# Out-projection accumulated onto a ScalarE copy in PSUM, two early products in row tiles, and a reworked end of the FFN

## The chip, the cores and the metric

The kernel runs on one core of one Trainium2 chip. The metric is the device time of one launch in microseconds. The kernel before took 1280.64 us (median of three runs, 1278.71 to 1283.99).

## The reference

One layer of a streaming encoder over 1024 tokens of width 1024, all in float32: sandwich RMSNorm, a token mixer with two head groups (a gated DeltaNet and a latent attention) whose outputs are concatenated, one output projection, and a squared-ReLU MLP with 4096 hidden columns. The part that the change touches is the second half of the layer:

```python
mixed = jnp.concatenate([o_gdn, o_mla], axis=-1) @ w_out[l]
x = x + rms_norm(mixed, mix_post_norm[l])
h = rms_norm(x, ffn_pre_norm[l])
f = jnp.square(jax.nn.relu(h @ w_up[l])) @ w_down[l]
x = x + rms_norm(f, ffn_post_norm[l])
```

## The kernel before, in words

Every float32 matrix product is done as three fp32r products (`mm3`, lines 207 to 209): each operand is split into a high part (a cast on ScalarE) and a low part (the difference, on VectorE). The tokens are eight blocks of 128, `t` = 0 to 7. TensorE's lines in the trace are mostly those of `mm3`, so the stages are told apart by tile names: `ps_out` is the out-projection, `ps_h2T` the transposes of its normalised rows, `ps_up` and `ps_dn` the two halves of the FFN.

**Out-projection.** The DeltaNet's share of it is computed during the attention and kept in SBUF as `part[t]`. What is left for a block is the attention's share: for each half of 512 columns four pairs, that is 12 matmuls, into a PSUM bank (`out_pairs`). `out_add` then adds the bank to `part[t]` on VectorE (line 1172) and squares the sum on ScalarE into the bank, with the row sums as a by-product (line 1173). Blocks 0 and 1 (`early`) are done at the end of the attention; blocks 2 to 7 take their banks from a pool of four (`psC`, tag `out`). `out_proj(t)` goes on with the norm: the sum of squares, the reciprocal root by a Sqrt on ScalarE and a Newton step in small VectorE operations (lines 155 to 172), the scaling by `rpost` (line 1245), the residual's add (1246), its store to `d_x1`, a second sum of squares on ScalarE (1249), and the scaling by `rffn` (1251). The residual `xt` shares a ring of six tiles (tag `g`) with other tiles.

**First half of the FFN.** It runs on a 2x2 scheme with seven products of half-size blocks in place of eight (the sums and differences T1 to T4 of the rows and S1 to S4 of the weights). `ffn_in(t)` transposes a block's rows on TensorE into one of two banks, and casts and splits them (`put`, lines 1268, 1273 and 1274). The products with the rows' first blocks, B11 and B21, need only token blocks 0 to 3; for every even `p` they are taken ahead as `filler(p)`, between the transposes of blocks 4 to 7, and their results are stored to DRAM. Each filler loads a block of `w_up` into a raw tile (`raw_of`: a ring of three, every fourth from the ring `g`), which stays in use until the filler's second result is stored. All these loads are chained in program order on SyncE's queue (`load_chained`, line 183). Row tiles, a ring of 16 (`mtile`, tag `m`), hold `part`, the attention's rows and later T2 and T4; they come free as blocks 4 to 7 are transposed. `up_pair(p)` then does the remaining products.

**Second half of the FFN.** The 56 steps (seven products, in the order 1, 7, 6, 5, 4, 3, 2, over eight blocks of hidden columns each) accumulate in four banks, one per pair of token blocks; `evict` adds a product to the rows `R` when its eight steps are done. In products 5, 4, 3 and 2 a half of the rows becomes final: it is squared on ScalarE (line 1570) and multiplied by the gain on GpSimd (`gains`, 1573). `final(t)` loads the residual `x1t` from DRAM into one of two tiles (1577), computes the root, and for each half scales and adds on VectorE (1583) and stores. In the last product the last `LASTU` steps are done block by block, so that the first blocks can be evicted while the others still accumulate.

The order of the instructions on each engine isn't that of the program text: a scheduler lists them by readiness on a simulated timeline and by program order among the ready ones, and the tiles' slots and semaphores follow from it. An engine then executes its list in that fixed order.

Of the kernel before, what the change touches and what calls it, by code (L numbers as in the profile page):

```python
# [8 lines left out]
F32 = mybir.dt.float32  # L9
F32R = mybir.dt.float32r  # L10
I32 = mybir.dt.int32
AF = mybir.ActivationFunctionType
ALU = mybir.AluOpType
# [4 lines left out]
P = 128  # L18
T = 1024
D = 1024  # L20
KT = D // P
NT = T // P
HALF = 512
# [4 lines left out]
NPAIR = MH // 2  # L28
# [76 lines left out]
def build(tc, a, out):  # L105
    nc = tc.nc
    mm = nc.tensor.matmul
# [7 lines left out]
    cp = pool(const_stack, "const")  # L115
# [14 lines left out]
    def psum(name, tag="ps"):  # L130
        return pp[0].tile([P, HALF], F32, name=name, tag=tag, bufs=pp[1][tag])
# [8 lines left out]
    ones = cp.tile([P, P], F32, name="ones")  # L140
    nc.vector.memset(ones, 1.0)
    cols = cp.tile([P, NCOL], F32, name="cols")
    cp.tile([P, 48], F32, name="edge_c")
    cur = [cp]

    def col(base, k):
# [2 lines left out]
    def small(shape, name, bufs=2):  # L149
        return cur[0].tile([P] + list(shape), F32, name=name, tag=name, bufs=bufs)  # L150
# [31 lines left out]
    def load_chained(dst, src):  # L182
        ld = nc.sync.dma_start(dst, src).ins
        if last_load:
            after(ld, last_load[0], "loads in the order of use")
        last_load[:] = [ld]
# [19 lines left out]
    def mm3(ps, lhs, rhs, start, stop, **kw):  # L206
        mm(ps, lhs[0], rhs[0], start=start, stop=False, **kw)  # L207
        mm(ps, lhs[0], rhs[1], start=False, stop=False, **kw)  # L208
        mm(ps, lhs[1], rhs[0], start=False, stop=stop, **kw)  # L209

    def cut(pair, *idx):
        return tuple(t[idx] for t in pair)
# [20 lines left out]
    d_x1 = scratch("d_x1", NT, P, D)  # L233
# [7 lines left out]
    R = ExitStack()  # L241
# [759 lines left out]
    first = pool(const_stack, "first")  # L1001
# [4 lines left out]
    mixT, gmix, part, mp = [None] * NPAIR, {}, [], []  # L1006
# [10 lines left out]
    def mtile(name, dt=F32R):  # L1017
        return mp[0].tile([P, T], dt, name=name, tag="m", bufs=16)
# [105 lines left out]
    def out_cols(w, i):  # L1124
        return cut(w[i // 2], slice(None), slice((i % 2) * HALF, (i % 2 + 1) * HALF))
# [36 lines left out]
                nc.scalar.copy(part[t][:, n * HALF : (n + 1) * HALF], ps)  # L1162
                yield

    def out_pairs(ps, t, n, pairs):

        for p in pairs:
            mm3(ps, cut(mixT[p], slice(None), slice(t * P, (t + 1) * P)), out_cols(w[n], p), p == 0, p == NPAIR - 1)

    def out_add(ps, t, n, ss):  # L1170
        h = part[t][:, n * HALF : (n + 1) * HALF]
        nc.vector.tensor_tensor(h, h, ps, op=ALU.add)
        nc.scalar.activation(ps, h, AF.Square, accum_out=ss[:, n : n + 1])

    early, ss1 = {}, {}
# [9 lines left out]
    for i in range(len(units) + LAG + 1):  # L1185
# [4 lines left out]
        if i < len(units):  # L1190
            h, q = units[i]
# [7 lines left out]
        if i >= LAG + 1:  # L1199
            h, q = units[i - LAG - 1]  # L1200
            if q % 2:
                attend(h, q // 2)
        if i == 58:
            w = [[stream(a["w_out"][n, 2 + k], spare=mix_pair if n and k else None) for k in range(2)] for n in range(2)]
# [7 lines left out]
    L.close()  # L1212
    psum_pool("psC", out=4, tr=2, ps=2)


    L = ExitStack()
    bp = pool(L, "blocks")
# [6 lines left out]
    gb = gtile("gpost")  # L1224
# [7 lines left out]
    def out_proj(t):  # L1232
        h = part[t]
        xt = gtile("xt")
        nc.sync.dma_start(xt, a["x"][t * P : (t + 1) * P, :])
        if t not in early:
            ss1[t] = small([2], "ss1")
            for n in range(2):
                ps = psum("ps_out", "out")
                out_pairs(ps, t, n, range(NPAIR))  # L1240
                out_add(ps, t, n, ss1[t])
        ss = ss1[t]
        nc.vector.tensor_scalar(ss[:, 0:1], ss[:, 0:1], ss[:, 1:2], None, op0=ALU.add)
        r = rstd_of(ss[:, 0:1], D, "rpost")
        nc.vector.scalar_tensor_tensor(h, h, r, gb, op0=ALU.mult, op1=ALU.mult)
        nc.vector.tensor_add(xt, xt, h)
        nc.scalar.dma_start(d_x1[t], xt)
        ss2 = small([1], "ss2")
        nc.scalar.activation(h, xt, AF.Square, accum_out=ss2)
        r2 = rstd_of(ss2, D, "rffn")  # L1250
        nc.vector.scalar_tensor_tensor(h, xt, r2, gf, op0=ALU.mult, op1=ALU.mult)
# [65 lines left out]
    def raw_of(src):  # L1317
        raws[0] += 1
        r = gtile("raw") if raws[0] % 4 == 3 else raw_tile()
        load_chained(r, src)  # L1320
        return r
# [22 lines left out]
        return p % 2 == 0  # L1344

    def filler(p):
        x = raw_of(a["w_up"][2 * p])
        w = split_of(x)
        yield
        ps = psum("ps_up")  # L1350
        for k in range(4):
            mm3(ps, k_slice(w, 0, k), moving(B11, k), k == 0, k == 3)
            if k == 1:
                yield
        nc.scalar.copy(x[:, first_half], ps)
        nc.scalar.dma_start(d_p1[p // 2], x[:, first_half])
        yield
        for k in range(4):
            mm3(ps, k_slice(w, 1, k), moving(B21, k), False, k == 3, skip_group_check=True)
            if k == 1:  # L1360
                yield
        square_of = x[:, second_half]
        nc.scalar.activation(square_of, ps, AF.Relu)
        nc.scalar.activation(square_of, square_of, AF.Square)
        nc.scalar.dma_start(act_block(p, 0), square_of)
        yield
# [185 lines left out]
    ep = pool(L, "down")  # L1552
# [11 lines left out]
    ssf = {}  # L1564
# [7 lines left out]
    def gains(t, s):  # L1572
        nc.gpsimd.tensor_tensor(R[t][:, s], R[t][:, s], gb2[:, s], op=ALU.mult)  # L1573

    def final(t):
        x1t = ep.tile([P, D], F32, name="x1t", tag="x1t", bufs=2)
        nc.sync.dma_start(x1t, d_x1[t])
        s1 = small([1], "ssr")
        nc.vector.tensor_tensor(s1, ssf[t][:, 0:1], ssf[t][:, 1:2], op=ALU.add)
        r = rstd_of(s1, D, "rfin")  # L1580
        for n, eng in enumerate((nc.sync, nc.scalar)):
            s = slice(n * HALF, (n + 1) * HALF)
            nc.vector.scalar_tensor_tensor(x1t[:, s], R[t][:, s], r, x1t[:, s], op0=ALU.mult, op1=ALU.add)
            eng.dma_start(out[t * P : (t + 1) * P, s], x1t[:, s])

    def add(dst, x, ps):
# [2 lines left out]
    def evict(i, t):  # L1589
        ps, r1, r2 = bank[t], R[t], R[t + 4]  # L1590
        a1, a2, b1, b2 = r1[:, first_half], r1[:, second_half], r2[:, first_half], r2[:, second_half]
        if i == 1:
            nc.scalar.copy(a1, ps)
        elif i == 7:
            add(b1, a1, ps)
        elif i == 6:
            add(a2, a1, ps)
            add(b1, b1, ps)
        elif i == 5:
            add(b2, b1, ps)  # L1600
            add(a2, a2, ps)
            squares(t + 4, HALF, D, 1)
            gains(t + 4, second_half)
        elif i == 4:
            add(b1, b1, ps)
            squares(t + 4, 0, HALF, 0)
            gains(t + 4, first_half)
            final(t + 4)
        elif i == 3:
            add(a2, a2, ps)  # L1610
            squares(t, HALF, D, 1)
            gains(t, second_half)
        else:
            add(a1, a1, ps)
            squares(t, 0, HALF, 0)
            gains(t, first_half)
            final(t)

    LASTU = 2
    for n in range(2):  # L1620
        d_prepare(n)
    for n, (i, u) in enumerate(steps):
# [79 lines left out]
```

## Time and profile before

| | us |
|---|---|
| median of three runs | 1280.64 |
| profiled execution, its own time | 1280.36 |
| its span, first to last instruction | 1278.6 |
| TensorE busy | 1222.9 (96%) |
| VectorE busy | 903.9 (71%) |
| ScalarE busy | 651.9 (51%) |
| GpSimd busy | 163.4 (13%) |
| mean granted TensorE clock | 0.985 of full speed |

Times in the trace are microseconds from the span's start. PE is TensorE, DVE VectorE, ACT ScalarE, POOL GpSimd, SP SyncE; a letter q behind a name is that engine's queue of DMA issues and waits. The granted clock is in parts of 2.4 GHz. A matmul's row is its own latency; successive matmuls overlap, so the pitch from start to start tells the rate.

### The profile page before, as it was taken

Reading aid. Unit: us, or ns where it says so; the run is one execution under the profiler, and the core shown is the slowest. Engines: PE = TensorE matmul, PEld = TensorE weight load, DVE = VectorE, ACT = ScalarE, POOL = GpSimd, SP = SyncE. Lnnn points to the kernel's source line nnn. Section 1 sums busy time; section 2 is a strip of 40 time slices with the busy share of each in tenths; the row PEclk is TensorE's granted clock in tenths of the full one; section 3 lists DMA queues with packets and bytes.
Section 4 is the critical chain, followed back from the end, with each engine's and each line's share of the span. In section 5 each row is a group of like instructions: output and inputs, shape, how many; then the busy total and the mean of one; then the engine's idle time right before and its main releaser. Section 6 shows DMA issues by size and latency. Waiting matters only on the chain.

```text
span 1278.6 us, 17685 instructions
## 1 busy us (share of the span) xinstructions
PE 1222.9 (96%) x6224; PEld 1035.5 (81%) x6224; DVE 903.9 (71%) x1779; ACT 651.9 (51%) x1189; POOL 163.4 (13%) x152
## 2 busy tenths in 40 slices
PE   7999999999889999999898999999999999999995
PEld 6978888899778878887686888888887888888884
DVE  7678889546556785686976777677656786776744
ACT  6567643425645786774555544444445433344431
POOL 1011011220044553430000000000000000011021
PEclk9999999999989999999898999999999999999998
DMA  5114535736342511124444455455449984555902
GB/s 233 47 61 149 186 119 194 214 86 176 97 139 87 161 50 31 42 67 148 157 164 158 148 201 196 162 206 188 174 154 410 365 295 148 193 165 202 343 19 98
DMA packets 111217, 205.71 MB, mean 161 GB/s; under 512 B 33557, under 2 KB 51989, under 8 KB 111130
## 3 DMA queue, kind: packets, MB, share of 16 engines
q1 hardware_dynamic: 94848, 176.09, 41.1%
q10 hardware_dynamic: 16282, 28.50, 6.0%
q8 instruction: 49, 0.80, 0.3%
q14 instruction: 38, 0.31, 0.1%
HBM read 143.07 MB, written 61.49 MB: 160 GB/s over the span
## 4 chain that ended last, share of the span: by engine, by line
PE 60%; DVE 5%; DMA 3%; ACT 2%; issue 1%; POOL 1%; SPq 0%; DVEq 0%; ACTq 0%; POOLq 0%
PE ps_up L207 8%; PE ps_up L209 8%; PE ps_up L208 8%; PE ps_dn L208 8%; PE ps_dn L209 8%; PE ps_dn L207 8%; PE ps_PT L1061 2%; PE ps_out L207 2%; PE ps_out L208 1%; PE ps_out L209 1%; PE ps_o L1080 1%; PE ps_sc L207 1%; PE ps_o L1079 1%; PE ps_sc L208 1%; PE ps_sc L209 1%
## 5 line engine op out<-in xcount | busy, mean ns | idle before, releaser
L1573 POOL TENSOR_TENSOR rows<-rows,gpost 128x512 f32<-128x512 f32 x16 | 23.9, 1512 | 654.8 <-ACT junk L1570 654.8
L209 PE MATMUL ps_proj<-hThi,wlo 128*128 128x512 f32 x192 | 75.1, 395 | 1.2 <-DVE wlo L199 1.2
L207 PE MATMUL ps_proj<-hThi,whi 128*128 128x512 f32 x192 | 76.0, 396 | 0.0
L208 PE MATMUL ps_proj<-hTlo,whi 128*128 128x512 f32 x192 | 76.0, 396 | 0.0
L1065 DVE TENSOR_TENSOR PTlo<-ps_PT,PThi 128x512 fp32r<-128x512 f32 (+2 forms) x96 | 52.0, 550 | 20.0 <-ACT PThi L1064 19.3
L1064 ACT CAST PThi<-ps_PT 128x512 fp32r<-128x512 f32 (+2 forms) x96 | 45.4, 481 | 29.7 <-PE ps_PT L1061 28.1
L1505 DVE TENSOR_TENSOR dlo<-draw,dhi 128x1024 fp32r<-128x1024 f32 x35 | 44.7, 1301 | 22.0 <-ACT dhi L1504 21.9
L208 PE MATMUL ps_dn<-dlo,dhi 128*128 128x512 f32 x144 | 56.0, 389 | 0.0
L209 PE MATMUL ps_dn<-dhi,dlo 128*128 128x512 f32 x144 | 56.0, 389 | 0.0
L207 PE MATMUL ps_dn<-dhi 128*128 128x512 f32 x144 | 55.5, 389 | 0.0
L1325 ACT CAST whi<-raw 128x1024 fp32r<-128x1024 f32 (+1 forms) x29 | 26.3, 906 | 54.7 <-PE ps_up L208 48.9
L1035 ACT ACTIVATE Pt<-ps_sc,nm 128x896 f32<-128x896 f32 (+3 forms) x64 | 48.0, 749 | 11.8 <-DVE nm L1033 7.6
L1504 ACT CAST dhi<-draw 128x1024 fp32r<-128x1024 f32 x35 | 36.1, 1048 | 34.1 <-issue 13.8
L1061 PE MATMUL ps_PT<-ident,Pt 128*128 128x128 f32 x288 | 46.6, 276 | 2.4 <-DVE PTlo L1065 1.2
L1033 DVE TENSOR_REDUCE nm<-ps_sc 128x1 f32<-128x896 f32 (+3 forms) x64 | 47.8, 750 | 1.2
L1040 POOL TENSOR_TENSOR Pt<-Pt,rs 128x128 f32<-128x128 f32 (+4 forms) x40 | 35.4, 885 | 89.1 <-DVE rs L1038 65.1
L199 DVE TENSOR_TENSOR wlo<-raw,whi 128x1024 fp32r<-128x1024 f32 (+1 forms) x27 | 33.7, 1251 | 17.5 <-ACT whi L198 14.9
L1079 PE MATMUL ps_o<-PThi,V 128*128 128x256 f32 (+1 forms) x160 | 41.2, 280 | 3.2 <-DVE o L1086 1.4
L209 PEld LDWEIGHTS ps_proj<-hThi,wlo 128*128 128x128 f32 x192 | 36.1, 188 | 9.2 <-DVE wlo L199 1.7
L208 PEld LDWEIGHTS ps_proj<-hTlo,whi 128*128 128x128 f32 x192 | 36.1, 188 | 7.4 <-issue 0.5
L207 PEld LDWEIGHTS ps_proj<-hThi,whi 128*128 128x128 f32 x192 | 36.1, 188 | 7.4 <-issue 0.5
L1080 PE MATMUL ps_o<-PTlo,V 128*128 128x256 f32 (+1 forms) x160 | 41.2, 300 | 0.0
(589 smaller groups left out, 3969.6 us busy)
## 6 DMA issues: line engine op xcount, KB each, us to landing
draw<-in_w_down_dram SPq DMA_DIRECT2D x47, 512.0 KB
draw<-d_act SPq DMA_DIRECT2D x41, 512.0 KB
raw<-in_w_up_dram SPq DMA_DIRECT2D x40, 512.0 KB
raw<-in_w_down_dram SPq DMA_DIRECT2D x17, 512.0 KB
raw<-in_w_qkvg_dram SPq DMA_DIRECT2D x16, 512.0 KB
d_act<-c SPq DMA_DIRECT2D x16, 512.0 KB
d_act<-s SPq DMA_DIRECT2D x16, 512.0 KB
raw<-d_act SPq DMA_DIRECT2D x15, 512.0 KB
```

Source lines behind the costliest of these rows:

```text
L207: mm(ps, lhs[0], rhs[0], start=start, stop=False, **kw)
L208: mm(ps, lhs[0], rhs[1], start=False, stop=False, **kw)
L209: mm(ps, lhs[1], rhs[0], start=False, stop=stop, **kw)
L1033: nc.vector.tensor_reduce(nm, ps[:, :npc, :w], axis=AX.XY, op=ALU.max, negate=True)
L1035: nc.scalar.activation(Pt[:, :n].rearrange("p (i w) -> p i w", i=npc), ps[:, :npc, :w], AF.Exp, bias=nm, scale=1.0, accum_out=sm)
L1061: transpose(ps[:, j * P : (j + 1) * P], Pt[:, b * P : (b + 1) * P], ident)
L1064: nc.scalar.copy(hi[:, :n, cs], ps3)
L1065: nc.vector.tensor_sub(lo[:, :n, cs], ps3, hi[:, :n, cs].bitcast(F32))
L1079: mm(ps[:, cs], V[h][:, b], hi[:, cs], start=(b == 0), stop=False)
L1080: mm(ps[:, cs], V[h][:, b], lo[:, cs], start=False, stop=(b == nb - 1))
L1504: nc.scalar.copy(hi, raw)
L1505: nc.vector.tensor_tensor(lo, raw, hi.bitcast(F32), op=ALU.subtract)
```

## The change

It has four parts. In the out-projection of blocks 2 to 7, ScalarE copies `part[t]` into the two banks, all 12 products of a half are accumulated onto the copy, ScalarE squares the bank directly, and VectorE's scaling by `rpost` reads the banks in two halves. Four matmuls ahead of it write each of the four banks once. Fillers 8 and 12 load into row tiles and not into the rings for raw blocks. At the end of the FFN the residual has four tiles, its load is issued from ScalarE's queue (for blocks 0 to 3 one product earlier than the block is finished), the last product's gain multiplication is done by VectorE into a free half of the rows, and the last three steps, not two, go block by block. The filler tile `edge_c` becomes 16 columns smaller.

```diff
--- before.py
+++ after.py
@@ -140,7 +140,7 @@
     ones = cp.tile([P, P], F32, name="ones")
     nc.vector.memset(ones, 1.0)
     cols = cp.tile([P, NCOL], F32, name="cols")
-    cp.tile([P, 48], F32, name="edge_c")
+    cp.tile([P, 32], F32, name="edge_c")
     cur = [cp]
 
     def col(base, k):
@@ -1162,10 +1162,11 @@
                 nc.scalar.copy(part[t][:, n * HALF : (n + 1) * HALF], ps)
                 yield
 
-    def out_pairs(ps, t, n, pairs):
-
+    def out_pairs(ps, t, n, pairs, onto=False):
+
+        kw = dict(skip_group_check=True) if onto else {}
         for p in pairs:
-            mm3(ps, cut(mixT[p], slice(None), slice(t * P, (t + 1) * P)), out_cols(w[n], p), p == 0, p == NPAIR - 1)
+            mm3(ps, cut(mixT[p], slice(None), slice(t * P, (t + 1) * P)), out_cols(w[n], p), p == 0 and not onto, p == NPAIR - 1, **kw)
 
     def out_add(ps, t, n, ss):
         h = part[t][:, n * HALF : (n + 1) * HALF]
@@ -1212,6 +1213,9 @@
     L.close()
     psum_pool("psC", out=4, tr=2, ps=2)
 
+    for _ in range(4):
+        mm(psum("ps_out", "out"), w[0][0][0][:, :P], w[0][0][0][:, :HALF], start=True, stop=True)
+
 
     L = ExitStack()
     bp = pool(L, "blocks")
@@ -1235,14 +1239,21 @@
         nc.sync.dma_start(xt, a["x"][t * P : (t + 1) * P, :])
         if t not in early:
             ss1[t] = small([2], "ss1")
-            for n in range(2):
-                ps = psum("ps_out", "out")
-                out_pairs(ps, t, n, range(NPAIR))
-                out_add(ps, t, n, ss1[t])
+            banks = [psum("ps_out", "out") for n in range(2)]
+            for n, ps in enumerate(banks):
+
+                other = h[:, n * HALF : (n + 1) * HALF]
+                nc.scalar.copy(ps, other)
+                out_pairs(ps, t, n, range(NPAIR), onto=True)
+                nc.scalar.activation(other, ps, AF.Square, accum_out=ss1[t][:, n : n + 1])
+        else:
+            banks = [h[:, :HALF], h[:, HALF:]]
         ss = ss1[t]
         nc.vector.tensor_scalar(ss[:, 0:1], ss[:, 0:1], ss[:, 1:2], None, op0=ALU.add)
         r = rstd_of(ss[:, 0:1], D, "rpost")
-        nc.vector.scalar_tensor_tensor(h, h, r, gb, op0=ALU.mult, op1=ALU.mult)
+        for n, ps in enumerate(banks):
+            s = slice(n * HALF, (n + 1) * HALF)
+            nc.vector.scalar_tensor_tensor(h[:, s], ps, r, gb[:, s], op0=ALU.mult, op1=ALU.mult)
         nc.vector.tensor_add(xt, xt, h)
         nc.scalar.dma_start(d_x1[t], xt)
         ss2 = small([1], "ss2")
@@ -1344,7 +1355,11 @@
         return p % 2 == 0
 
     def filler(p):
-        x = raw_of(a["w_up"][2 * p])
+
+        m = p >= 8 and p % 4 == 0
+        x = mtile(f"raw{p}", F32) if m else raw_of(a["w_up"][2 * p])
+        if m:
+            load_chained(x, a["w_up"][2 * p])
         w = split_of(x)
         yield
         ps = psum("ps_up")
@@ -1572,15 +1587,21 @@
     def gains(t, s):
         nc.gpsimd.tensor_tensor(R[t][:, s], R[t][:, s], gb2[:, s], op=ALU.mult)
 
-    def final(t):
-        x1t = ep.tile([P, D], F32, name="x1t", tag="x1t", bufs=2)
-        nc.sync.dma_start(x1t, d_x1[t])
-        s1 = small([1], "ssr")
-        nc.vector.tensor_tensor(s1, ssf[t][:, 0:1], ssf[t][:, 1:2], op=ALU.add)
+    x1 = {}
+
+    def load_x1(t):
+        x1[t] = ep.tile([P, D], F32, name="x1t", tag="x1t", bufs=4)
+        nc.scalar.dma_start(x1[t], d_x1[t])
+
+    def final(t, first=None):
+        rows = R[t][:, first_half] if first is None else first, R[t][:, second_half]
+        x1t = x1.pop(t)
+        s1 = small([1], "ssr", 4)
+        nc.vector.tensor_scalar(s1, ssf[t][:, 0:1], ssf[t][:, 1:2], None, op0=ALU.add)
         r = rstd_of(s1, D, "rfin")
         for n, eng in enumerate((nc.sync, nc.scalar)):
             s = slice(n * HALF, (n + 1) * HALF)
-            nc.vector.scalar_tensor_tensor(x1t[:, s], R[t][:, s], r, x1t[:, s], op0=ALU.mult, op1=ALU.add)
+            nc.vector.scalar_tensor_tensor(x1t[:, s], rows[n], r, x1t[:, s], op0=ALU.mult, op1=ALU.add)
             eng.dma_start(out[t * P : (t + 1) * P, s], x1t[:, s])
 
     def add(dst, x, ps):
@@ -1605,18 +1626,21 @@
             add(b1, b1, ps)
             squares(t + 4, 0, HALF, 0)
             gains(t + 4, first_half)
+            load_x1(t + 4)
             final(t + 4)
         elif i == 3:
             add(a2, a2, ps)
             squares(t, HALF, D, 1)
             gains(t, second_half)
+            load_x1(t)
         else:
             add(a1, a1, ps)
             squares(t, 0, HALF, 0)
-            gains(t, first_half)
-            final(t)
-
-    LASTU = 2
+
+            nc.vector.tensor_tensor(b1, a1, gb2[:, first_half], op=ALU.mult)
+            final(t, b1)
+
+    LASTU = 3
     for n in range(2):
         d_prepare(n)
     for n, (i, u) in enumerate(steps):
```

## Rows read from the trace of the kernel before

**Rows 1.** Stages: length, busy us of PE, PEld, DVE, ACT, POOL; granted clock; DMA.
```profile
623.00:632.00 9.00, 2.90 (x18) 2.47 (x17) 9.00 (x28) 4.00 (x13) 0.00 (x0) 0.85 0.21 61
632.00:640.00 8.00, 8.00 (x29) 6.45 (x30) 8.00 (x16) 4.37 (x9) 0.00 (x0) 0.75 0.80 310
670.00:684.00 14.00, 8.59 (x38) 6.23 (x37) 7.89 (x14) 8.05 (x17) 0.00 (x0) 0.76 0.43 169
696.00:1264.00 568.00, 566.46 (x2500) 468.31 (x2497) 394.02 (x478) 248.93 (x313) 21.02 (x14) 1.00 0.58 205
```

**Rows 2.** TensorE's waits, 560 to 720 us: total us, times, longest.
```profile
PE ps_h2T L1268 <- DVE rpost_v L172: 6.1, 1, 6.1
...
PE ps_h2T L1268 <- DVE B22lo L1274: 1.5, 1, 1.5
```

**Rows 3.** Chain of waits, 585 to 700 us: start, us, what; its shares first.
```profile
by line: PE ps_up L207 13.9%; PE ps_up L209 13.2%; PE ps_up L208 13.2%; PE ps_h2T L1268 7.6%; DMA xt<-in_x_dram 5.2%; DVE part L1251 4.5%; DVE part L1172 4.1%; issue 4.0%; DVE wlo L1326 3.6%; DMA raw<-in_w_up_dram 3.2%; DVE xt L1246 3.1%; A
...
589.66 5.94 DMA xt<-in_x_dram
...
628.60 1.28 DVE part L1251
...
675.51 3.70 DMA raw<-in_w_up_dram
```

**Rows 4.** Groups by line and shape, 587 to 700 us: count | busy, mean ns | idle.
```profile
L1172 DVE TENSOR_TENSOR part<-part,ps_out 128x512 f32<-128x512 f32 x13 | 8.7, 679 | 0.5 <-PE ps_out L209 0.4
...
L1173 ACT ACTIVATE ps_out<-part 128x512 f32<-128x512 f32 x14 | 8.3, 596 | 2.8 <-DVE rffn L156 1.5 <-DVE part L1172 1.3
```

**Rows 5.** Timeline of the out-projection, several engines: start, us, engine, what [idle before].
```profile
587.24 0.45 PE L207 MATMUL ps_out<-whi,first_hi 128*128 128x512 f32 x1
...
590.05 1.28 ACT L155 ACT_TABLE_LOAD   x1 [1.24 <-POOL mixlo L944]
...
599.17 0.50 PE L207 MATMUL ps_out<-whi,first_hi 128*128 128x512 f32 x1 [0.79 <-ACT ps_out L1173]
...
604.85 1.27 DVE L1245 SCALAR_TENSOR_TENSOR part<-part,rpost,gpost 128x1024 f32<-128x1024 f32 x1
```

**Rows 6.** Timeline of the tail, several engines.
```profile
1243.45 1.22 DVE L1505 TENSOR_TENSOR first_lo<-draw,first_hi 128x1024 fp32r<-128x1024 f32 x1 [3.08 <-ACT first_hi L1504]
...
1256.20 0.69 DVE L1587 TENSOR_TENSOR rows<-rows,ps_dn 128x512 f32<-128x512 f32 x1 [11.52 <-PE ps_dn L209]
...
1258.56 0.27 DVE L159 TENSOR_SCALAR rfin_t<-rfin,rfin_v 128x1 f32<-128x1 f32 x1
...
1263.93 0.39 PE L209 MATMUL ps_dn<-first_hi,wlo 128*128 128x512 f32 x1
...
1265.77 1.40 DVE L1583 SCALAR_TENSOR_TENSOR x1t<-rows,rfin,x1t 128x512 f32<-128x512 f32 x2
...
1269.55 0.33 SPq L1577 DMA_DIRECT2D x1t<-d_x  x1
...
1270.48 0.27 DVE L159 TENSOR_SCALAR rfin_t<-rfin,rfin_v 128x1 f32<-128x1 f32 x1
...
1270.98 0.21 DVE L165 TENSOR_SCALAR rfin<-rfin,rfin_t 128x1 f32<-128x1 f32 x1
...
1274.21 1.41 DVE L1583 SCALAR_TENSOR_TENSOR x1t<-rows,rfin,x1t 128x512 f32<-128x512 f32 x2 [3.01 <-DMA x1t<-d_x]
```

**Rows 7.** Timeline of loads (SyncE's queue) and of TensorE's products with w_up.
```profile
647.01 2.29 SPq L183 DMA_DIRECT2D raw<-in_w_up_dram  x2
...
649.40 0.37 SPq L1417 DMA_DIRECT2D c<-d_p  x1
...
657.54 0.39 PE L207 MATMUL ps_up<-B11hi,whi 128*128 128x512 f32 x1
...
660.89 0.33 SPq L1418 DMA_DIRECT2D s<-d_act  x1
...
680.34 0.80 PE L207 MATMUL ps_up<-B11hi,whi 128*128 128x512 f32 x1 [1.08 <-ACT whi L1325]
```

## The prediction

> **What bounds the kernel now.** I read the busy shares by stage first. From 696 to 1264 us TensorE is busy for 566.46 of 568 us at full clock [rows 1], and its last matmul ends at 1263.93 + 0.39 = 1264.32 [rows 6]. So what TensorE gains or loses ahead of 696 comes out one for one at the end, and relief for other engines in that long stretch is worth nothing. Three places are left where time can move.
>
> Place A is the out-projection, 587 to 640. TensorE sits idle for 6.1 us in one piece ahead of a transpose, put down to VectorE's rpost_v [rows 2], and for 0.8 us behind a square [rows 5]. VectorE is busy without a gap from 623 to 640, and TensorE's granted clock is 0.85 over 9 us and 0.75 over 8 us there [rows 1]: after the idle piece it ran for a while at its 1.2 GHz level. That cost at most 0.15 x 9 + 0.25 x 8 = 3.35 us; I take 3.1, since a little of it fell into idle time. Place A holds 0.8 + 6.1 + 3.1 = 10.0 us. The chain of waits says whose time it is: it comes in by the residual's load (5.94 us from 589.66) and then runs over VectorE and ScalarE until block 3's scaling at 628.60; the out-adds alone are 4.1% of that window of 115 us, 4.7 us or eight pieces of 0.6 [rows 3].
>
> Place B is 670 to 684. TensorE is busy for 8.59 of 14 us at a clock of 0.76 [rows 1]. It waits 1.5, 1.4 and 1.4 us for the low part of a transpose (one row stands for the three [rows 2]) and 1.1 us for the high part of a w_up block, whose load started only at 675.51 and took 3.70 us [rows 3, 7]. Slow clock: 0.24 x 14 = 3.4 us at most, I take 2.9. Sum 5.4 + 2.9 = 8.3 us. TensorE had only transposes left there, because its next products lacked weights.
>
> Place C is the tail: from 1264.32 to the end of the span at 1278.6, 14.3 us of norm and output of the last blocks.
>
> **Out-projection's parts in PSUM (place A).** Removed from VectorE: 12 adds of 0.68 us (blocks 2 to 7, two halves). They follow one another every 0.60 us, so 7.2 us, of which 4.7 are on the chain for certain and the rest feeds squares on it [rows 3, 4]. Added: two half scalings in place of one of 1.27 us [rows 5]; a half that reads PSUM is nearest to the add's 0.68, so 0.09 us a block, 0.4 us up to block 3. Block 3 should come about 6.5 us sooner (4.3 to 6.8), which takes up the idle piece of 6.1 us, and with it the 3.1 us of slow clock.
>
> Added on ScalarE: 12 copies of 128x512 into PSUM. None is in the trace; the square that writes the same tile from SBUF takes 0.60 us [rows 4], so 7.2 us. Below they are hidden wholly, above each stands ahead of its products. ScalarE is busy for 4.37 of 8 us where VectorE is full [rows 1], so I count only the copies ahead of block 2 and behind a freed bank, in the next two terms.
>
> Added on TensorE: four matmuls at the pitch of block 2's and 3's 48, (599.17 - 587.24 - 0.79) / 48 = 0.23 us [rows 5]: 0.9 us. Block 2's products, which started at 587.24, now wait for them and for a copy. ScalarE loads a table from 590.05 for 1.28 us, after 1.24 us of waiting in its queue for GpSimd [rows 5]. A copy in front of that costs block 2 some 1.5 us, one behind it 590.05 + 1.28 + 0.60 - 587.24 = 4.7 us. Behind block 2 on TensorE stands only block 3, as every transpose needs VectorE first. I take 3.2 us, about the middle, as no row is nearer to either end.
>
> The wait that is new: a bank stays in use until the scaling has read it, where the square after the add freed it before. Four banks are two blocks. The cycle of one pair is 0.60 (copy) + 24 x 0.23 (products) + 0.79 (square and its sum) + 1.7 (small operations, from the tail's chain below) + 1.36 (two halves) = 10.0 us; two pairs overlap, so 5.0 us a block against TensorE's 5.5: no wait, if VectorE takes each scaling at once. So far it did not. Block 2's products ended at about 592.8 and its scaling began at 604.85 [rows 5], 12 us later where 2.5 would do. Much of that was the adds in front of it and the residual's load, which lands at 595.6 [rows 3] and stays as it is. Bounds 0 and 16 us (the latter under rival 1); I take 2, near the low end, since the cycle has slack and the next stage's products can fill holes once block 3 is in.
>
> Place A: -10.0 + 0.9 + 3.2 + 2.0 = -3.9 us.
>
> **Two early products in row tiles (place B).** The products p = 8 and 12 take their weights from the ring of row tiles, so the later loads find a buffer sooner in the two other rings. Now p = 8 is loaded at 647.01; up_pair's first row tile comes free at 649.40, its second at 660.89 [rows 7]. Under the change p = 8 is ahead of those in the order and gets the first, 2.4 us later than now, hidden because its product starts at 657.54 [rows 7], 10 us after the load. p = 12 gets the second, at about 661 in place of 675.51, and p = 14, next in the chain of loads, comes with it. From load to product it was 680.34 - 675.51 = 4.8 us [rows 7], so p = 12 is ready at 666, before TensorE runs dry at 670. Then products lie between the transposes, and the waits (5.4) and the slow clock (2.9) go. What is late next: the first load of up_pair(0), which inherits the starved buffer; 2 x 24 x 0.23 = 11 us of products cover it, but with transposes in between I leave 2 us. Bounds: all 8.3 gone, or nothing if the tile is late. Place B: -8.3 + 2.0 = -6.3 us. Further on the rings only turn in another order: nothing, as TensorE does not wait there [rows 1].
>
> **End of the FFN (place C).** The last block's root is ready at 1270.98 + 0.21; then it waits 3.0 us for its residual, whose load could start only at 1269.55, when one of two buffers had been written out [rows 6]. With four buffers, loaded a step of eight products earlier, that wait goes. Three products per block at the end in place of two set the blocks 18 x 0.23 = 4.1 us apart in place of 2.8, and a block's own chain is hardly longer: for the first block of the tail, the only one undisturbed, 1256.20 to 1258.56, then 0.71 us to the root (as from 1270.48 to 1271.19), a gap of 0.1 and two halves in 1.40, together 4.6 us [rows 6]. GpSimd's gains leave the chain; VectorE's product with the gain in their place lies beside ScalarE's square. So the last block's second half ends at 1264.32 + 4.6 + 0.5 (behind the block before) = 1269.4 where it is 1274.21 + 1.41 = 1275.6 now. The 3.0 us after that (issue and transfer) stay. Place C: -6.2 us; bounds -3.0 (only the load's wait) and -6.7 (no block in the way). The group of three needs its last split at 1264.32 - 72 x 0.23 + 12 x 0.23 = 1250.5; it is done at 1243.45 + 1.22 [rows 6]. Loads moved into ScalarE's queue take 0.33 us each to issue [rows 6], in steps where TensorE never waits. Nothing there.
>
> **Sum.** -3.9 - 6.3 - 6.2 = -16.4 us against the profiled execution's own 1280.36 us (the span and 1.8 around it), which lies 0.3 below the median shown: 1264.0 us.
>
> **Rivals.** (1) Banks held too long: slower. If each scaling still comes 12 us after its block's products, block 4 starts at 604.85 + 1.36 + 0.6 = 606.8 in place of 599.17, 7.6 us of standing; block 5 follows without a wait, block 6 stands for another 8.5, block 7 for none: 16.1 us. If nothing fills it, A turns into -10.0 + 4.1 + 16.1 = +10.2, B keeps its waits, C gives -6.2: 1284 us. It decides from 12 us of standing. For it: VectorE is full from 623 to 640. Against it: the adds that go were in front of those scalings. The Trainium skill speaks for it: "PSUM — Partial Sum Buffer", section "Summary: rules for kernel authors", asks to evacuate promptly, and here a bank's last reading moves to later. No run here shows the longer hold yet.
>
> (2) Only the tail pays: A's saving goes into its new waits, and B stays limited by the transposes, for which three of its four waits are. 1280.4 - 6.2 = 1274 us.
>
> (3) The row tile comes late: if p = 8 gets the tile of 660.89 and not that of 649.40, its product moves from 657 to 666, the chained loads follow, and B loses about 2 us where it would win: -3.9 + 2 - 6.2, 1272 us.
>
> (4) A runs without its new waits, VectorE keeping ahead: A -8, B -8, C -6.5: 1258 us.
>
> **How the numbers follow.** Forecast (1259 to 1270) 0.58, (1) 0.07, (2) 0.12, (3) 0.10, (4) 0.13. The range of 8 in 10 goes from 1255 (the low bounds, -9.1 - 8.3 - 6.7, and 1 us of scatter between runs) to 1275, which takes in (2) and (3). About 0.5%, 6.4 us, is what a measurement can tell from no change here. Faster than 1274.2: the forecast, (3), (4) and nearly half of (2), 0.86; within it the rest of (2) and a little of (1), 0.08; slower 0.06.
>
> **What would show it.** No adds of part and ps_out for blocks 2 to 7, and block 3's scaling by rffn near 622 in place of 628.60; no idle piece over 3 us on TensorE between 600 and 640; the load of p = 12 near 661 and no cluster of waits near 675; the last matmul near 1254, and 8 us from it to the end of the span in place of 14.3. It is wrong if TensorE stands for more than 6 us ahead of ps_out (rival 1), if the last matmul hardly moves (rival 2), or if the last scaling still waits for x1t.

## The result, and the profile after

The changed kernel takes 1274.2 us (median of 9 runs, 1269.56 to 1276.31) against 1280.88 us for the kernel before beside it (9 runs); the ratio is 0.9943, with a 95% interval of 0.9926 to 0.9959. That is -7.3 us where -16.4 was forecast, and it is the time of rival (2), in which only the tail pays. The profiled execution has a span of 1272.5 us.

The stages of the kernel after, with the stage behind place B added (columns as in [rows 1]):

```profile
623.00:632.00 9.00, 5.91 (x29) 4.51 (x28) 8.06 (x18) 7.16 (x14) 0.00 (x0) 0.94 0.50 176
632.00:640.00 8.00, 8.00 (x26) 6.36 (x26) 8.00 (x19) 2.53 (x5) 0.00 (x0) 0.64 0.19 77
670.00:684.00 14.00, 14.00 (x73) 11.60 (x72) 3.24 (x7) 5.83 (x13) 0.00 (x0) 1.00 0.55 199
684.00:696.00 12.00, 6.16 (x31) 4.48 (x30) 10.56 (x18) 8.40 (x16) 0.00 (x0) 0.71 0.47 161
696.00:1264.00 568.00, 567.29 (x2494) 468.69 (x2492) 397.08 (x491) 246.12 (x310) 20.13 (x12) 1.00 0.57 204
```

Against [rows 1], the hole from 670 to 684 is gone: TensorE is full at full clock. But 684 to 696 is now half empty and slow, and from 632 to 640 the clock is lower than before. How 684 to 696 looked in the kernel before:

```profile
684.00:696.00 12.00, 11.52 (x61) 9.38 (x60) 7.94 (x14) 7.34 (x15) 0.00 (x0) 1.00 0.27 87
```

There it was busy for 11.52 of 12 us. The hole has moved by one stage; it has not closed. TensorE's longest waits in the kernel after, 560 to 720 us (total us, times, longest), where the 6.1 us of [rows 2] are gone and five others stand:

```profile
PE ps_out L207 <- ACT ps_out L1246: 2.8, 4, 1.3
PE ps_up L207 <- ACT B11hi L1284: 2.5, 1, 2.5
PE ps_h2T L1279 <- DVE T2lo L1285: 2.2, 1, 2.2
PE ps_h2T L1279 <- DVE T4lo L1285: 2.1, 1, 2.1
PE ps_h2T L1279 <- DVE T3lo L1285: 0.8, 1, 0.8
```

The first two are place A's. The first is the wait for ScalarE's copies: 0.53 us ahead of block 2, behind the four set-up matmuls (line 1217), then 1.32, 0.45 and 0.45 us ahead of blocks 4 to 6:

```profile
586.10 0.92 PE L1217 MATMUL ps_out<-whi 128*128 128x512 f32 x3
...
588.22 0.50 PE L207 MATMUL ps_out<-whi,first_hi 128*128 128x512 f32 x1 [0.53 <-ACT ps_out L1246]
...
600.74 0.50 PE L207 MATMUL ps_out<-whi,first_hi 128*128 128x512 f32 x1 [1.32 <-ACT ps_out L1246]
```

The timeline of the kernel after shows where the second comes from (several engines):

```profile
622.04 1.28 DVE L1262 SCALAR_TENSOR_TENSOR part<-xt,rffn,gffn 128x1024 f32<-128x1024 f32 x1
...
626.81 1.04 PE L1279 MATMUL ps_h2T<-ident,part 128*128 128x128 f32 x8
...
628.23 1.04 ACT L1336 CAST first_hi<-raw 128x1024 fp32r<-128x1024 f32 x1 [1.60 <-DMA raw<-in_w_up_dram]
...
629.76 0.57 ACT L1284 CAST B11hi<-ps_h2T 128x512 fp32r<-128x512 f32 x1
...
630.38 0.73 PE L207 MATMUL ps_up<-B11hi,whi 128*128 128x512 f32 x2 [2.54 <-ACT B11hi L1284]
```

Block 3's scaling comes at 622.04, as forecast (622), 6.6 us sooner than in [rows 3]. Its transposes, ready at 623.3, stand on TensorE behind block 7's products until 626.81. Their cast then stands on ScalarE behind the cast of a w_up block that waits 1.60 us for its load, and behind block 7's square. The other three waits are place B's:

```profile
677.06 0.60 PE L1279 MATMUL ps_h2T<-ident,t 128*128 128x128 f32 x4
...
677.74 10.64 SPq L183 DMA_DIRECT2D raw<-in_w_up_dram  x4
...
687.59 0.68 DVE L1413 TENSOR_TENSOR sums<-raw 128x512 f32<-128x512 f32 x1
...
690.62 1.09 PE L1279 MATMUL ps_h2T<-ident,part 128*128 128x128 f32 x4 [2.23 <-DVE T2lo L1285]
...
694.56 0.78 PE L207 MATMUL ps_up<-T1hi,wv_hi 128*128 128x512 f32 x1
```

The products of p = 12 and 14 end at 684.5; the load of pair 0 is issued only at 677.74, when the transposes of a "t" have read the buffer that it inherits, and its sums run at 687.59 on a VectorE that is busy for 10.56 of 12 us. Last, the tail:

```profile
1263.37 0.69 DVE L1608 TENSOR_TENSOR rows<-rows,ps_dn 128x512 f32<-128x512 f32 x1 [0.41 <-PE ps_dn L209]
...
1265.04 1.41 DVE L1604 SCALAR_TENSOR_TENSOR x1t<-rows,rfin,x1t 128x512 f32<-128x512 f32 x2
...
1266.36 0.15 DVE L172 TENSOR_SCALAR rfin_v<-ssr 128x1 f32<-128x1 f32 x1
...
1268.04 1.42 DVE L1604 SCALAR_TENSOR_TENSOR x1t<-rows,rfin,x1t 128x512 f32<-128x512 f32 x2
```

The last matmul ends at 1263.34, 1.0 us sooner than in [rows 6], where 1254 was forecast; the span ends 9.2 us behind it where it was 14.3.

### The profile page after: what moved, and what is told of

Read it like the earlier page. It is cut to its first block, busy times and chain, and to the rows that moved or that the text cites. A ratio compares the mean times of both kernels' runs of the same rounds, so it can differ in the third digit from the quotient of the medians.

```text
span 1272.5 us, 17691 instructions
## 1 busy us (share of the span) xinstructions
PE 1223.9 (96%) x6228; PEld 1035.0 (81%) x6228; DVE 901.6 (71%) x1779; ACT 656.4 (52%) x1201; POOL 160.0 (13%) x148
## 4 chain that ended last, share of the span: by engine, by line
PE 63%; DVE 3%; ACT 3%; DMA 2%; issue 1%; POOL 0%; SPq 0%; ACTq 0%; DVEq 0%; POOLq 0%
PE ps_up L208 8%; PE ps_up L209 8%; PE ps_up L207 8%; PE ps_dn L208 8%; PE ps_dn L209 8%; PE ps_dn L207 8%; PE ps_PT L1061 2%; PE ps_out L207 2%; PE ps_out L209 2%; PE ps_out L208 2%; PE ps_o L1080 1%; PE ps_sc L207 1%; PE ps_o L1079 1%; PE ps_sc L208 1%; PE ps_sc L209 1%
## 5 line engine op out<-in xcount | busy, mean ns | idle before, releaser
L1588 POOL TENSOR_TENSOR rows<-rows,gpost 128x512 f32<-128x512 f32 x12 | 20.1, 1703 | 617.8 <-ACT junk L1585 617.8
L199 DVE TENSOR_TENSOR wlo<-raw,whi 128x1024 fp32r<-128x1024 f32 (+1 forms) x27 | 33.8, 1254 | 18.1 <-ACT whi L198 15.5
L1061 PEld LDWEIGHTS ps_PT<-ident,Pt 128*128 128x128 f32 x288 | 34.0, 140 | 8.6 <-issue 2.5
```

What stands on the lines that cost most here:

```text
L1061: transpose(ps[:, j * P : (j + 1) * P], Pt[:, b * P : (b + 1) * P], ident)
```

## Experiments

**The parts alone.** e1 is the kernel before with the end of the FFN of after, e2 with the out-projection of after, e3 with the new filler, e4 with nothing but the residual's four buffers and early loads. The edits below are shown in part.

```diff
# e4, against before
-        x1t = ep.tile([P, D], F32, name="x1t", tag="x1t", bufs=2)
-        nc.sync.dma_start(x1t, d_x1[t])
+        x1t = x1.pop(t)
+        x1[t] = ep.tile([P, D], F32, name="x1t", tag="x1t", bufs=4)   # load_x1, called in steps 4 and 3
+        nc.scalar.dma_start(x1[t], d_x1[t])
```

e1: 

> Only the end of the FFN is changed (four x1t buffers, no GpSimd, groups of three). Theory (only the tail pays): the last matmul stays at 1264.3 and the span ends 9 us behind it instead of 14.3, so 1276 us, ratio 0.996, and the whole change is no faster than this kernel. Rival (each part pays something and the parts disturb each other): the tail alone gives about -5 as well, but the whole change (-6.7) is then the sum of smaller gains, so this kernel would be at 1278 or more, ratio 0.998.

e2: 

> Only the out-projection's parts go into PSUM. Theory: the saving of 10 us at 587 to 640 goes into idle pieces ahead of ps_out (0.5 + 1.3 + 0.45 + 0.45), an idle piece of 2 to 3 us behind block 3's transposes and slow clock after it: 1280 us, within 1.5 us of before, ratio 0.999 to 1.001. Rival (the two early parts pay apart and hide each other in the whole): -4 us, ratio 0.997, last matmul near 1260. Second rival (banks held): +4 or more.

e3: 

> Only the two early products take row tiles. Theory: TensorE is full from 670 to 684 and then waits for the transposes' low parts from 684 to 696 by about as much as it waited before: first product by T1 near 696, 1280 us, ratio 0.999 to 1.001. Rival (this part pays by itself): -6 us, ratio 0.995, first product by T1 near 690.

e4: 

> Of the end of the FFN only the four x1t buffers with their early loads; GpSimd's gains and the groups of two stay. Theory (three terms make the tail's gain, the load's wait is one of them): the wait for x1t goes from 3.0 us to none, the span ends 11 to 12 us behind the last matmul, -3 us, ratio 0.998. Rival (GpSimd's gains or VectorE's queue end right behind the load): -1 us or less, 13 us behind the last matmul.

Measured, as ratios to the kernel before: e1 0.9959 (0.9944 to 0.9973), which is -5.3 us; e2 1.0011 (0.9998 to 1.0023); e3 1.0009 (1.0001 to 1.0018); e4 0.9978 (0.9966 to 0.9990), -2.8 us. Only the tail pays; the two other parts are worth nothing alone. The theory had "no faster" for the whole than for e1; it is 2 us faster, within both intervals. The three parts add up to -2.7 us and the whole has -7.3: 4.6 us apart, a little more than the four intervals allow (3.4 us, their half widths added as squares), so the two front parts do better together than apart. What they hide from each other is the subject of the next runs. e3's stages show its hole moved as in the whole:

```profile
670.00:684.00 14.00, 13.08 (x70) 10.85 (x68) 3.41 (x7) 7.08 (x17) 0.00 (x0) 1.00 0.44 145
684.00:696.00 12.00, 4.96 (x26) 4.01 (x27) 10.40 (x18) 7.32 (x15) 0.00 (x0) 0.72 0.54 192
```

and e2's waits from 587 to 640 show place A refilled (the profiled execution of e2 is the slowest of its twelve, 1286.0 us, so its rows show a long wait ahead of block 4):

```profile
PE ps_out L207 <- ACT ps_out L1246: 4.5, 4, 3.1
PE ps_up L207 <- ACT B11hi L1284: 2.6, 1, 2.6
```

**The tail with groups of two.** e12 is e1 with `LASTU = 2`.

> The end of the FFN alone, as in e1, but with groups of two in place of three. Theory (three terms: the load's wait -2.8 as in e4, the spacing of the blocks, GpSimd): blocks come 2.8 us apart where VectorE needs about 3.8 for one, so the last block stands behind three others by 3 us: 12 us behind the last matmul, ratio 0.998. Rival (spacing is free, the load and GpSimd are all): 9 us behind it, 0.996 as e1.

Measured: 0.9956 (0.9944 to 0.9967), the same as e1. The rival holds: the groups of three are worth nothing that can be measured. The tail's 5.3 us are the load's wait, 2.8 (e4), and 2.5 for the rest of its edits. Of these the main one takes GpSimd out of the chain; no run has it alone, so its share is not shown.

**Lifting one limit at a time.** These start from the changed kernel. e5 orders two queues around block 3; e6 takes pair 0's first block out of the ring that the transposes hold; e7 sets the last eight transposes between the last products (a dependency without a semaphore that only fixes the order on the engine); e8 is e6 and e7.

```diff
# e5: on TensorE, block 7's second half behind block 3's transposes; on ScalarE, the cast of p = 4 behind block 3's
+                if (t, n) == (NT - 1, 1):
+                    after(first, put_all[7][0], "block 3 first")
+        if ring[0] == 3:
+            after(cast, put_all[7][1], "block 3 first")
# e6: load_up(0)
+            first = mtile("raw_0", F32)
+            load_chained(first, a["w_up"][0])
# e7: one transposed piece ahead of a product of p = 12 or 14
+    turns = {(12, 4): 20, (12, 5): 21, (12, 7): 22, (14, 0): 23, (14, 1): 24, (14, 3): 25, (14, 4): 26, (14, 6): 27}
+            after(ins, put_all[turns[p, k]][0], "transposes first")
```

e5: 

> The changed kernel with block 3 let past in two queues: its transposes stand on TensorE between block 7's two halves, and its two casts on ScalarE ahead of the cast of a w_up block that is still being loaded. Theory (place A's gain was eaten by that order, and what TensorE wins there only lengthens its wait for pair 0 in place B): idle of 2.54 + 0.55 us near 630 and the slow clock of 632 to 640 go, the early products end near 679 in place of 684.5, but the first product with T1 stays at 692 to 694.5; 0 to -2 us against the changed kernel, 1272 to 1274, ratio 0.993 to 0.994. Rival (each place pays by itself): -6 us, 1268, ratio 0.9895, first product with T1 near 688.5. Second rival (the order was not the cause): idle near 630 stays over 2 us.

e6: 

> The changed kernel with the first w_up block of pair 0 in a row tile, so that its load does not wait for a buffer that the last blocks' transposes read. Theory (two limits in place B: pair 0's weights, and the transposes through two banks): the load is issued near 664 in place of 677.7, the sums are done before 682, VectorE has 6 us less to do from 684 to 694, the eight last transposes run at about 1 us each and the first product with T1 starts near 691.5: -3 us, ratio 0.992. Rival (the transposes alone): first product with T1 stays near 694.5, 0 us. Second rival (weights alone): it starts at 688, -6 us.

e7: 

> The changed kernel with the last eight transposes set between the products of p = 12 and 14 on TensorE. Theory (two limits): no wait for a low part over 1 us from 684 to 692, but TensorE then waits for pair 0's weights, whose split ends near 692: first product with T1 near 692, -2 us, ratio 0.993. Rival (the transposes alone were the limit): first product with T1 near 688.5, -6 us or more with the clock, ratio 0.9895.

e8: 

> Both: pair 0's block in a row tile and the last transposes between the products. Theory (two limits, both gone): first product with T1 near 688.5, TensorE full from 640 on, no slow clock from 690 to 699, -7 us against the changed kernel, 1267, ratio 0.989. Rival (place B has a third limit, or the gain is given back when pair 1's weights are late after 700): -3 us or less.

Measured: e5 0.9955 (0.9942 to 0.9968), e6 0.9957 (0.9943 to 0.9970), e7 0.9934 (0.9918 to 0.9950), e8 0.9925 (0.9912 to 0.9938); the changed kernel has 0.9943. e5 is the telling one. Its idle of 2.54 us and the slow clock near 632 are gone (TensorE 8.00 of 8 us at 1.00), and the last matmul of its early products starts at 676.55 where the changed kernel's starts at 684.13: 6.6 us sooner, counted from block 2's first product (587.21 and 588.22). But the first product with T1 comes only 2.1 us sooner, counted so, because the last transposes wait (TensorE, VectorE and ScalarE of e5):

```profile
676.55 0.39 PE L209 MATMUL ps_up<-B21hi,first_lo 128*128 128x512 f32 x1
...
685.36 2.51 ACT L1339 CAST whi<-raw 128x1024 fp32r<-128x1024 f32 x3
...
687.29 2.95 DVE L1342 TENSOR_TENSOR wlo<-raw,whi 128x1024 fp32r<-128x1024 f32 x3
...
687.77 0.36 ACT L1286 CAST T4hi<-ps_h2T 128x256 fp32r<-128x256 f32 x1
...
690.17 0.41 DVE L1287 TENSOR_TENSOR T4lo<-ps_h2T,T4hi 128x256 fp32r<-128x256 f32 x1
...
690.73 1.08 PE L1281 MATMUL ps_h2T<-ident,part 128*128 128x128 f32 x4 [4.18 <-DVE T4lo L1287]
...
691.46 0.77 PE L207 MATMUL ps_up<-T1hi,wv_hi 128*128 128x512 f32 x1
```

Of 6.6 us won ahead of 677, 4.5 are lost again by 691, and in the median time nothing is left (the profiled execution is the fastest of its six). e6 and e7 alone are worth nothing or 1 us, neither clear of no change. In e6 the first product with T1 starts at 693.87, where its theory had 691.5; in e7 it starts at 692.40 as forecast, but behind a wait of 2.41 us for a low part, where its theory had none over 1 us. e8, forecast at -7, gave -2.3, and the intervals leave 2.7 either way: its rival holds, and e5's rows name a third limit. Pair 0's splits stand in front of the last transposes' in two queues. The transposes for T4 end at 686.55, but their cast runs on ScalarE at 687.77, behind three casts of pair 0; it ends at 688.13, but the low part for which the bank waits runs on VectorE at 690.17, behind three of pair 0.

**All limits of place B.** e9 is e5 and e8 together; e10 adds the order of pair 0's later splits, given on VectorE, which holds back their casts on ScalarE too; e11 adds the order by which block 2's banks come free ahead of the residual's adds.

```diff
# e10, in prepare(): pair 0's third block behind the last low part
+        if p == 0:
+            after(late, put_all[-1][-1], "low parts first")
# e11, in out_proj(): xt + h of blocks 0 and 1 behind block 2's scaling
+        if t in early:
+            after(add_, block2[0], "banks first")
```

e9: 

> Block 3 let past (as in e5), pair 0's block in a row tile and the last transposes between the products (as in e8). Theory (place A's gain is lost in place B for as long as place B ends by pair 0's weights and the transposes): with both lifted, the 4 us that e5 won ahead of 684 come out at the end: ratio 0.989, 1266 to 1267, first product with T1 near 689. Rival (VectorE's order is a third limit: pair 0's splits stand in front of the last low parts): first product with T1 near 691.5, ratio 0.992, no better than e8.

e10: 

> e9, and on VectorE the splits of pair 0 that its third and later products read come behind the last low part. Theory (VectorE's order is the third limit): no wait of TensorE for a low part over 1.2 us from 676 to 692, first product with T1 near 688, ratio 0.988, 1265. Rival: the same as e9 within 0.001, since the two transposes' banks and ScalarE's casts set the pace.

e11: 

> e10, and block 2's scalings, which free its banks, come on VectorE ahead of the adds of blocks 0 and 1, which wait for the residual's load. Theory (the bank of block 4 waits for that load by VectorE's order): the wait of 1.3 to 3.1 us of block 4's copy goes to 0.5 or less, place A ends 1 to 2.5 us sooner, ratio 0.001 to 0.002 below e10. Rival: block 3's scaling gets later by as much, and nothing is won.

Measured: e9 1267.23 us, 0.9890 (0.9873 to 0.9907); e10 1264.51 us, 0.9866 (0.9849 to 0.9883); e11 1265.18 us, 0.9871 (0.9858 to 0.9884). What e5 won for nothing comes out once place B's limits are lifted, as the theory of e9 has it: e9 is 4.5 us below e8. That the order of pair 0's splits was the third limit shows in the rows. From e9 to e10 TensorE's waits for low parts from 664 to 692 fall from 5.8 to 2.8 us, and the first product with T1 comes 4.1 us sooner, with block 2's first product at 588.13 and 588.16 (first row e9, second e10):

```profile
690.28 0.39 PE L207 MATMUL ps_up<-T1hi,wv_hi 128*128 128x512 f32 x1
```

```profile
686.16 0.39 PE L207 MATMUL ps_up<-T1hi,wv_hi 128*128 128x512 f32 x1
```

In time it is 3.1 us, which is as much as the two intervals leave open. e10 beats both kernels: -17 us against before (four runs). Its stages:

```profile
623.00:632.00 9.00, 8.68 (x43) 6.62 (x42) 9.00 (x17) 7.44 (x16) 0.00 (x0) 1.00 0.51 178
632.00:640.00 8.00, 8.00 (x39) 6.62 (x38) 7.89 (x21) 3.91 (x8) 0.00 (x0) 1.00 0.33 131
670.00:684.00 14.00, 11.43 (x64) 8.45 (x62) 9.74 (x20) 8.60 (x19) 0.00 (x0) 1.00 0.36 125
684.00:696.00 12.00, 12.00 (x57) 9.92 (x56) 7.31 (x12) 5.56 (x9) 0.00 (x0) 1.00 0.45 164
```

TensorE is idle for 2.9 us in the four, at full clock. e11 fell to its rival. Block 4's wait is gone, and block 5 has one of 3.04 us in its place (TensorE and VectorE of e11):

```profile
598.61 3.48 DVE L1262 TENSOR_TENSOR xt<-xt,part 128x1024 f32<-128x1024 f32 x3
...
609.72 0.80 PE L207 MATMUL ps_out<-whi,first_hi 128*128 128x512 f32 x1 [3.04 <-ACT ps_out L1246]
```

The adds that were moved, and what follows from them, now stand ahead of block 3's scaling at 608.30, which frees block 5's banks.

**Are the parts' savings in e10, or only the orders'?** e13 is e10 with the out-projection of before (without e5's orders, which belong to it), e14 is e10 with the filler of before.

```diff
# e13, the out-projection's adds again on VectorE
+                ps = psum("ps_out", "out")
+                out_pairs(ps, t, n, range(NPAIR))
+                out_add(ps, t, n, ss1[t])
# e14
+        x = raw_of(a["w_up"][2 * p])
```

e13: 

> e10 without the out-projection in PSUM (parts added on VectorE as before, and no set-up matmuls): the tail, the two row tiles, pair 0's block in a row tile, the last transposes between the products and VectorE's order stay. Theory (part A's saving is really in e10, once its stage's end is no longer set by pair 0 and the transposes): the idle piece of 6.1 us near 628 and the slow clock come back, less the 4.5 us of idle and set-up matmuls that e10 still has there: 5 us above e10, 1269 to 1270, ratio 0.991. Rival (the new orders are the whole gain): 0.9866 as e10.

e14: 

> e10 without the two early products in row tiles (their blocks in the two rings as before); all else stays, the part in PSUM too. Theory (part B's saving is really in e10): TensorE lacks weights near 670 again, 3 to 6 us above e10, ratio 0.989 to 0.991, with a wait for a w_up cast over 1 us between 665 and 690. Rival (pair 0's block in a row tile already frees the rings): within 0.001 of e10.

Measured: e13 0.9915 (0.9899 to 0.9930), 6.3 us above e10; e14 0.9931 (0.9915 to 0.9948), 8.3 us above. The differences have 95% intervals of 3 us either way. Both rivals are out: neither is as fast as e10. e13's theory holds; it has the old idle piece again. e14 has the old hole from 670 to 684 again, at a clock of 0.63, but it lost more than the 3 to 6 us of its theory, and its longest wait for a w_up cast is 0.7 us where over 1 was expected; TensorE's longer waits there are three for low parts, of 1.4, 1.3 and 1.1 us. One row of each kernel:

```profile
632.81 1.94 PE L1268 MATMUL ps_h2T<-ident,part 128*128 128x128 f32 x8 [6.09 <-DVE rpost_v L172]
```

```profile
670.00:684.00 14.00, 9.41 (x35) 6.88 (x35) 7.79 (x14) 7.25 (x16) 0.00 (x0) 0.63 0.54 207
```

The first product with T1 is at 694.68 in e13 and at 695.64 in e14, and at 686.16 in e10 (block 2 starts at 587.29, 589.30 and 588.16): taking out either part loses most of it. These profiled executions flatter the difference a little: those of e13 and e14 are the slowest of their six, that of e10 is faster than its median. Alone the two parts were worth nothing (e2, e3); taken out of e10, where the other limits are lifted, they cost 6.3 and 8.3 us. This is how savings behave that must all be there for the end of a stage to move. Two things stay open. The 6.3 us are the price of the part in PSUM together with e5's two orders, and e8, which has the part without these orders (and without that of pair 0's splits), is no faster than e13 (0.9925 against 0.9915). And no run has the orders and the buffer with neither part.

## Why the prediction was wrong, step by step

**The frame.** The prediction treated A and B as two holes of TensorE and added what closing each would give. The rows show one stage from 587 to 696, which ends with the first product with T1. Three chains lead there: TensorE's own work, pair 0's weights (load, sums, splits), and the last blocks' transposes through two banks, ScalarE's casts and VectorE's low parts. In the kernel before, all three ended within 3 us of 696: the last early product at 694.8, the split of pair 0 that the first product with T1 reads at 693.2, the last transposes at 696.3. A saving in one is then worth nothing alone: e2, e3, e5 and e6 are four such savings, and none changed the time by more than 2 us. What the first product with T1 gains does come out at the end: from there to the end of the last matmul it is 568.2 us before, 568.8 after and 566.7 in e10. So "one for one" holds from that product on, and not for what one place gains ahead of it. From e1 to e10 there are 0.0093, 11.9 us. That this is near the 10.2 forecast for A and B is luck in part: it took four orders and a buffer that the forecast did not have.

**Place A, forecast -3.9, measured +1.4 (-0.3 to 2.9) in e2.** What was removed came out as forecast: no adds, block 3's scaling at 622.04. Of what was added, the set-up matmuls and block 2's copy take 2.1 us together, from 586.10 to 588.22 (forecast 0.9 + 3.2; the copies ran ahead of the table load, the low one of the two cases), the bank waits of blocks 4 to 6 1.32 + 0.45 + 0.45 = 2.2 (forecast 2.0; 3.1 + 0.9 in e2, where VectorE waited 1.41 us for the residual's load first). Together 4.3 of the 6.1 allowed. The step that failed is "takes up the idle piece of 6.1 us, and with it the 3.1 us of slow clock": 2.54 + 0.55 us of idle and (1 - 0.64) x 8 + (1 - 0.94) x 9 = 3.4 us of slow clock, at most, came back, by the orders on TensorE and ScalarE, which e5 lifts. 4.3 + 3.1 + 3.4 = 10.8 against the 10.0 removed. The prediction said of TensorE's queue that behind block 2 stood only block 3, and it listed nothing of ScalarE's queue behind the casts. On this the Trainium skill, "PSUM — Partial Sum Buffer", section "Engine vs sequencer instructions", says that ScalarE's, VectorE's and GpSimd's queues are strictly first in, first out. The trace agrees: block 3's cast, whose transposes ended at 627.85, ran at 629.76, behind a cast that waited 1.60 us for its load.

**Place B, forecast -6.3, measured +1.2 (0.1 to 2.3) in e3.** The early part held: all four of the loads p = 8 to 14 were issued by 657.4 (p = 12 was forecast for 661, against 675.51 before), and there is no cluster of waits near 675:

```profile
646.44 10.99 SPq L183 DMA_DIRECT2D raw<-in_w_up_dram  x4
```

The step that failed is "what is late next": the 11 us of products were to cover pair 0's load and leave 2 us. They were used up by 684.5. In the kernel before, these same products, late as they were, covered pair 0's preparation and the last transposes from 680 to 695 (11.52 of 12 us busy). Now there are 12 - 6.16 = 5.8 us of idle, and the slow clock lasts beyond 696:

```profile
694.00:698.00 4.00, 4.00 (x12) 3.32 (x12) 4.00 (x7) 1.16 (x3) 0.00 (x0) 0.50 0.65 225
698.00:702.00 4.00, 4.00 (x16) 3.19 (x16) 3.93 (x7) 1.22 (x2) 0.00 (x0) 0.84 0.00 0
```

It costs 0.50 x 4 + 0.16 x 4 = 2.6 us there, and 0.7 in the 1.65 us that TensorE is busy from 688 to 694 at 0.50 to 0.75. That makes 9.1 us, for the 8.3 won and the 0.5 that was there; the term put at 2 us was the one mis-sized. That pair 0's load waits for transposes, and the order of its splits, are not in the prediction, which reads no row between 684 and 696.

**Place C, forecast -6.2, measured -5.3 (e1).** The mechanism was right and the sizes nearly so. The load's wait was put at 3.0 and is 2.8 (e4). The last block's chain, from its add at 1263.37 to the end of its second half at 1269.46, takes 6.1 us and not 4.6 + 0.5: a product with the gain and the halves of the block before (1265.04, 1.41 us) stand in its way on VectorE, so that the sum done at 1265.1 is followed by the next step only at 1266.36. The spacing of 4.1 us, on which the forecast rested the block's free way, is worth nothing that can be measured (e12).

**The rivals.** (2) came true in its time, and in its reasons in part; it had 0.12. The transposes in place B are there, beside pair 0's weights, which it did not name; place A's new waits are 4.3 of 10.8 us, and the rest is order and slow clock. Rival (1) did not come true: the waits for the copies into the banks are 2.8 us in all and 4.6 at most (e14), not 16. The Trainium skill's advice to evacuate promptly ("PSUM — Partial Sum Buffer", "Summary: rules for kernel authors") is borne out in its sign by those waits, but they did not decide.

## What to carry to other kernels

Before the closing of a hole is counted, write down what the work that fills it covers where it stands now, and read the rows there: work moved earlier uncovers what it hid. Where several chains end within a few us of each other, the saving is that of the chain that is last afterwards, so such edits are tried together, and taken out of the full set one by one. A chain that got faster can be worth nothing until its instructions also stand ahead of slower ones in each queue that it passes; here four fixed orders and one buffer turned -7 into -17 us.

## What the runs showed of the hardware

A 128x1 sum of two operands in SBUF on VectorE takes 0.15 to 0.16 us, but took 1.09 with GpSimd multiplying beside it; both end together at 1270.7 (kernel e4, two engines):

```profile
1269.12 1.61 POOL L1573 TENSOR_TENSOR rows<-rows,gpost 128x512 f32<-128x512 f32 x1 [1.39 <-ACT junk L1570]
...
1269.66 1.09 DVE L1584 TENSOR_TENSOR ssr<-ssf 128x1 f32<-128x1 f32 x1
```

The kernel before has such a sum of 1.09 us in its tail too. In that of after, where GpSimd does not run, the sum is a tensor_scalar of 0.21 to 0.22 us. This may be a part of the 2.5 us that e1 has over e4; no run has it alone. The ScalarE copy of 128x512 into PSUM, of which no row of before existed, takes 0.58 us; the square that stood for it has 0.60.

Executions of one front differ more than expected: from the first product of block 2 to the first with T1 it is 108.85 us in the kernel before, 109.40 in e1 and 111.58 in e12, whose code is the same up to there but for the size of `edge_c`. Between e1 and e12 most of it comes from block 4's first product, whose chain goes back to the residual's load (first row e1, second e12):

```profile
598.35 0.50 PE L207 MATMUL ps_out<-whi,first_hi 128*128 128x512 f32 x1 [1.40 <-ACT ps_out L1173]
```

```profile
598.34 0.50 PE L207 MATMUL ps_out<-whi,first_hi 128*128 128x512 f32 x1 [2.04 <-ACT ps_out L1173]
```

TensorE waits 0.6 us longer in e12, and behind that wait its granted clock was 0.69 from 600 to 604, where it was 1.00 in e1. VectorE had waited 1.27 us for the load in e1 and 1.89 in e12. So a difference of 2 us in that stage between two profiles shows nothing by itself, and the verdicts above go by the timed ratios. After which idle pieces the clock falls stays open: behind 2.54 us in the changed kernel it did (0.64 from 632 to 640), and in e7 it did behind 2.46 us ahead of 631.90 (0.57 from 632 to 636) and did not behind 2.41 us ahead of 687.35 (1.00 from 684 to 696).
